# Gate and up of the second FFN by seven half-size products instead of eight, on normalised activations

## The chip, the cores and the metric

One core of a Trainium2 chip. The metric is the device time of one execution in microseconds (us), the median of several runs.

## The reference

One step of a decoder layer over 544 tokens: 512 of a prompt and 32 of eight decoding sequences.

```python
def rmsnorm(x, g):
    xf = x.astype(jnp.float32)
    y = xf * lax.rsqrt(jnp.mean(xf * xf, axis=-1, keepdims=True) + EPS)
    return (y * g.astype(jnp.float32)).astype(x.dtype)

def swiglu(x, w_gate, w_up, w_down):
    return (jax.nn.silu(x @ w_gate) * (x @ w_up)) @ w_down

x = x + 0.5 * swiglu(rmsnorm(x, ffn1_norm), ffn1_w_gate, ffn1_w_up, ffn1_w_down)
x = x + mixer(rmsnorm(x, mix_norm))     # convolution group and sparse attention group
x = x + 0.5 * swiglu(rmsnorm(x, ffn2_norm), ffn2_w_gate, ffn2_w_up, ffn2_w_down)
```

x has 1024 features, the hidden layer of an FFN 2816 = 22 x 128. Everything is float32.

## The kernel before

The activations lie transposed in SBUF, features on the partitions: x is [128, 8 k-tiles, 544 tokens]. A float32 product is made of three products in the format fp32r: each operand is split into a high part (ScalarE's copy rounds it) and a low part (VectorE subtracts the high part from the source), and high x high, high x low and low x high are accumulated in PSUM.

`stream` brings 128 columns of a weight matrix into one of three staging buffers (`wst`, `WB = 3`), and splits them into `whi` and `wlo` (L166, L171), which go round three slots of one buffer each. `wmm` then runs, for each of the 8 k-tiles, three kinds of product and two halves of the tokens (272 columns each): 48 matmuls for a unit of 128 hidden features.

`ffn` walks over the hidden tiles f = 0 to 21 in three blocks (`BLOCKS`: 8, 8 and 6 tiles). Within a block it makes, for each f, a gate unit G and an up unit U, and `hidden` evicts both with the factor R = 1 / root mean square of each token (L276: `t<-G,R`, `u<-U,R`), applies silu on ScalarE (L278), multiplies (L280) and splits the result into `hh` and `hl` (L281, L282). Then it runs the down projection of the block: 8 chunks Y of output features, each over the block's 6 or 8 hidden tiles, added to x by L330. In the first FFN the same code runs; the diff leaves that FFN alone.

Before the second FFN stands the output projection of the mixer, `w_out(1)`: 8 chunks Yo, added to x by L1236. After each chunk `done` squares it (`sq`, `S`) and splits it, with the norm's gain, into the `xh` and `xl` of the second FFN (L207, L208). The sum of squares is complete after the eighth chunk; `rms_from_S` and `spread` then give R on all partitions (L260). Since R scales the columns of a product, the units of f = 0 run before R is there.

The order of the instructions on each engine is fixed when the kernel is built: a scheduler takes, on each engine, the ready instruction that comes first in the program (with offsets for some parts). So G's matmuls of f = 0 lie among those of Yo. GpSimd does nothing in the second FFN.

After each output chunk of the last block `done2` transposes it (`yT`, `yS`), copies it out of PSUM (`yn`) and writes it to DRAM in pieces.

Of the kernel before, what the change touches and what calls it, by code (L numbers as in the profile page):

```python
# [7 lines left out]
F32 = mybir.dt.float32  # L8
# [49 lines left out]
KTB = 3  # L58
PSC = 1
# [58 lines left out]
class Trunk:  # L118
# [36 lines left out]
    def stream(self, srcs, n, m, kind="", slot=None):  # L155
        """fp32 weights [128, n, m] from DRAM, as the two float32r parts, in the given or the next place of three."""
# [25 lines left out]
    def wmm(self, unit, parts, act, cuts=HALVES, which=(0, 1)):  # L182
        """unit[:, i, :] = W^T act over all k-tiles, for the ith cut of the tokens; W stationary."""
# [10 lines left out]
    def fmm(self, name, parts, act, n):  # L194
        """two PSUM banks, one per half of the tokens: W^T act over n k-tiles."""
# [35 lines left out]
    def rms(self, ssq):  # L231
        """sums of squares [128 tokens, 5 tiles] -> rn, 1 / root mean square."""
# [19 lines left out]
    def spread(self):  # L252
        """R [128, T]: the row of rn on every partition."""
# [9 lines left out]
    def ffn(self, wg, wu, wd, done, late=False):  # L263
# [3 lines left out]
        def hidden(f, G, U):  # L267
            """G, U: one PSUM tile of equal halves, or (columns, PSUM) pairs."""
# [95 lines left out]
    def begin_units(self):  # L364
        """loads and transposes the activations; the first gate and up units, by halves of the tokens as these come in."""
        nc, tc, i = self.nc, self.tc, self.i
        with tc.tile_pool(name="init", bufs=1) as ip, tc.high_priority(offset=FIRST):
# [13 lines left out]
            def weights(w, n):  # L381
                """w's first 128 columns in n runs of k-tiles: for each a function that loads it, fp32 and the two parts."""
# [57 lines left out]
            def mms(unit, w, hf, order="01234567" * 2):  # L440
                """the high parts of the weights at a k-tile's first mention, the low ones at its second."""
# [112 lines left out]
    def rope(self, v, i, n, nh, kind):  # L554
        """partial rotary on v [n tokens, nh, 64] of token tile i."""
# [32 lines left out]
    def load_half(self, pieces, m, ks=(4, 4), slots=(0, 1)):  # L588
        """w_in columns in runs of ks k-tiles, [128, k, m] each; pieces: (offset in tile, first column, width)."""
# [717 lines left out]
    def mixer(self):  # L1307
        nc, tc, i = self.nc, self.tc, self.i
        self.idx_cols = [([(0, C_QI, 256)], 256), ([(0, C_QI + 256, 328)], 328, KS, (2, 0, 1))]
        with tc.tile_pool(name="mid", bufs=1) as mp:  # L1310
# [124 lines left out]
            for c, _ in enumerate(self.w_out(1, act)):  # L1435
                done(c)
# [79 lines left out]
```

## Time and profile before

| what | us |
|---|---|
| median of 3 runs | 1278.44 |
| lowest and highest of them | 1274.17, 1284.3 |
| span of the profiled execution, first to last instruction | 1270.2 |
| median of the runs less that span | 8.2 |
| second FFN in the profiled execution, G of f = 2 to the last Y | 890.3 to 1265.3 |

The profiled execution's own time is not listed beside its span; only the three runs have one. A row of the trace names the line of the kernel, the engine (PE TensorE, DVE VectorE, ACT ScalarE, POOL GpSimd), the operation, what is written from what, and its shape. Matmuls are pipelined: the record of one is longer than the distance to the next. DVE instructions overlap a little in the same way, so that the distance from start to start is the price in a queue.

### The profile page before, as it was taken

To read this page: it belongs to the slowest core of one execution; us is meant where nothing else is said; L and a number is where in the kernel's file an instruction comes from. 1 tells how busy PE (TensorE), PEld (TensorE's weight loads), DVE (VectorE), ACT (ScalarE), POOL (GpSimd) and SP (SyncE) were. 2 spreads that over 40 slices of the span, in tenths; PEclk is the share of its full clock that TensorE was granted. 3 is DMA by queue.
4 is the path that set the end of the run, shared out by engine and by line. 5 is a ranking of instruction groups with operands and counts; after the bars stand their busy time and mean duration, and the time that the engine had idled before them with its cause. 6 is when DMAs were issued, how large, how long until landed. Compare 5 with 4: busy or idle time off the path is not lost.

```text
span 1270.2 us, 22873 instructions
## 1 busy us (share of the span) xinstructions
PE 1230.0 (97%) x9629; PEld 1112.8 (88%) x9629; DVE 640.4 (50%) x1230; ACT 456.4 (36%) x696; POOL 209.3 (16%) x319
## 2 busy tenths in 40 slices
PE   9999999999999999899989989999999999999998
PEld 8999999999999747776667545789999999999998
DVE  5444334433446216999999753265443344433442
ACT  6332122212224464456525556244222122222222
POOL 3200000000000646665413231310000000000000
PEclk9999999999999999999999999999999999999999
DMA  7422332332222553245224443543223323322322
GB/s 231 133 85 84 93 90 84 92 92 84 86 73 69 179 178 106 68 138 169 68 61 140 161 151 124 167 141 113 87 84 93 91 84 87 96 85 84 91 75 74
DMA packets 184363, 136.10 MB, mean 107 GB/s; under 512 B 5706, under 2 KB 172434, under 8 KB 184260
## 3 DMA queue, kind: packets, MB, share of 16 engines
q1 hardware_dynamic: 171700, 91.62, 24.7%
q0 software_dynamic: 11904, 42.26, 10.3%
q8 instruction: 76, 1.25, 0.4%
q10 hardware_dynamic: 656, 0.76, 0.2%
q14 instruction: 27, 0.22, 0.1%
HBM read 131.66 MB, written 2.96 MB: 106 GB/s over the span
## 4 chain that ended last, share of the span: by engine, by line
PE 83%; DVE 10%; DMA 2%; issue 2%; ACT 1%; POOL 1%; DVEq 0%; ACTq 0%; POOLq 0%
PE Y L191 20%; PE U L191 20%; PE G L191 19%; PE Yo L130 4%; DVE flip L829 3%; PE KTp L134 2%; PE lg L130 2%; PE nat L130 2%; DMA ckn<-in_cache_k,ik 2%; PE O L130 2%; PE ssc L130 1%; PE plg L130 1%; PE pO L130 1%; DVE pw L928 1%; PE gc L130 1%
## 5 line engine op out<-in xcount | busy, mean ns | idle before, releaser
L166 ACT ACTIVATE whi<-wst 128x1024 fp32r<-128x1024 f32 (+3 forms) x173 | 172.7, 999 | 582.6 <-PE Y L191 181.2
L171 DVE TENSOR_TENSOR wlo<-wst,whi 128x1024 fp32r<-128x1024 f32 (+3 forms) x156 | 180.7, 1158 | 26.8 <-ACT whi L166 23.1
L191 PE MATMUL Y<-hh,wlo 128*128 128x272 f32 (+2 forms) x704 | 147.6, 288 | 0.0
L191 PE MATMUL Y<-hh,whi 128*128 128x272 f32 (+2 forms) x704 | 147.4, 289 | 0.0
L191 PE MATMUL Y<-hl,whi 128*128 128x272 f32 (+2 forms) x704 | 147.1, 288 | 0.0
L191 PE MATMUL U<-xh,whi 128*128 128x272 f32 x688 | 142.0, 287 | 1.5 <-DVE t L274 1.5
L191 PE MATMUL U<-xh,wlo 128*128 128x272 f32 x688 | 141.6, 288 | 0.0
L191 PE MATMUL U<-xl,whi 128*128 128x272 f32 x688 | 141.3, 287 | 0.0
L191 PE MATMUL G<-xh,whi 128*128 128x272 f32 x656 | 135.6, 287 | 0.0
L191 PE MATMUL G<-xl,whi 128*128 128x272 f32 x656 | 135.0, 287 | 0.0
L191 PE MATMUL G<-xh,wlo 128*128 128x272 f32 x656 | 134.9, 288 | 0.0
L276 DVE TENSOR_TENSOR u<-U,R 128x544 f32<-128x544 f32 x43 | 31.2, 725 | 160.2 <-PE U L191 160.2
L191 PEld LDWEIGHTS Y<-hl,whi 128*128 128x128 f32 x704 | 111.4, 188 | 0.0
L191 PEld LDWEIGHTS Y<-hh,whi 128*128 128x128 f32 x704 | 111.1, 188 | 0.0
L191 PEld LDWEIGHTS Y<-hh,wlo 128*128 128x128 f32 x704 | 110.7, 189 | 0.0
L330 DVE SCALAR_TENSOR_TENSOR x<-Y,x 128x544 f32<-128x544 f32 x46 | 33.3, 725 | 152.2 <-PE Y L191 152.2
L191 PEld LDWEIGHTS U<-xh,whi 128*128 128x128 f32 x688 | 107.1, 188 | 1.6 <-ACT whi L166 1.6
L191 PEld LDWEIGHTS U<-xl,whi 128*128 128x128 f32 x688 | 107.5, 188 | 0.0
L191 PEld LDWEIGHTS U<-xh,wlo 128*128 128x128 f32 x688 | 107.1, 189 | 0.0
L169 POOL TENSOR_TENSOR wlo<-wst,whi 128x1024 fp32r<-128x1024 f32 (+2 forms) x17 | 34.4, 2025 | 423.4 <-ACT whi L166 422.8
L191 PEld LDWEIGHTS G<-xl,whi 128*128 128x128 f32 x656 | 102.6, 188 | 0.0
L191 PEld LDWEIGHTS G<-xh,whi 128*128 128x128 f32 x656 | 102.2, 188 | 0.0
(330 smaller groups left out, 2235.0 us busy)
## 6 DMA issues: line engine op xcount, KB each, us to landing
wst<-in_ffn_w_up SPq DMA_DIRECT2D x44, 512.0 KB, 3.7
wst<-in_ffn_w_gate SPq DMA_DIRECT2D x43, 512.0 KB
wst<-in_ffn_w_down SPq DMA_DIRECT2D x32, 512.0 KB, 4.1
wst<-in_w_in SPq DMA_DIRECT2D x16, 512.0 KB, 4.0
wst<-in_ffn_w_down SPq DMA_DIRECT2D x16, 384.0 KB, 3.5
xn<-in_x_prompt SPq DMA_DIRECT2D x4, 512.0 KB
wst<-in_w_in SPq DMA_DIRECT2D x8, 256.0 KB, 8.9
wst<-in_w_out SPq DMA_DIRECT2D x8, 256.0 KB, 2.6
```

The costliest lines, as they stand in the source:

```text
L130: ins = self.nc.tensor.matmul(*args, **kw)
L134: ins = self.nc.tensor.transpose(*args)
L166: nc.scalar.activation(hi, st, AF.Copy)
L169: nc.gpsimd.tensor_tensor(lo, st, hi.bitcast(F32), op=ALU.subtract)
L171: nc.vector.tensor_sub(lo, st, hi.bitcast(F32))
L191: self.nc.tensor.matmul(unit[:, i, :c1 - c0], a[:, k, :], b[:, k, c0:c1], start=k == 0 and j == 0, stop=k == n - 1 and j == 2)
L276: nc.vector.tensor_mul(dst.rearrange("p (a b) -> p a b", a=2), src[:, :, :HT], self.R.rearrange("p (a b) -> p a b", a=2))
L330: nc.vector.scalar_tensor_tensor(xc, Y[:, :, :HT], 0.5, xc, op0=ALU.mult, op1=ALU.add)
L829: V.tensor_scalar(junk, src, cand[:, k:k + 1], None, op0=ALU.is_ge, op1=ALU.add, accum_out=cnt[:, k:k + 1])
L928: nc.vector.scalar_tensor_tensor(W, t, wcol, W, op0=ALU.mult, op1=ALU.add)
```

## The change

Gate and up of the second FFN get a function of their own, `ffn_late`. The tiles f = 0 and 1 are made as before. From f = 2 on two neighbouring tiles are made together: the weights of the pair are a 2 x 2 matrix of blocks (two tiles of hidden features, two halves of the 1024 input features), the activations another one (two halves of the input features, two halves of the tokens), and their product is made by the Winograd form of Strassen's algorithm, 7 products of 4 k-tiles and 272 columns in place of 8. `factors` loads the two tiles, builds four sums of weight blocks on GpSimd and splits the seven left factors. `right` multiplies the activations by the gain and by R (so that the pairs need no R at the eviction), forms four differences on GpSimd and splits the seven right factors, once. `unit` runs the products and adds them up. The three constants are SB = 1 (one buffer for the sums of weights), ZB = 1 (one for the results) and EVICT = "vector". The split activations of f = 0 and 1 move to the memory of `hh` and `hl`, the block of four right factors takes that of the mixer's `xh` and `xl`, and later the output tiles `yn` and `ys` take it.

```diff
+    def factors(self, srcs, nk):
...
+        (a11, a12), (a21, a22) = [(t[:, 0], t[:, 1]) for t in st]
+        def parts(src, n, eng):
+            slot, self.slot = self.slot, (self.slot + 1) % 3
...
+            nc.scalar.activation(hi, src, AF.Copy)
+            eng.tensor_tensor(lo, src, hi.bitcast(F32), op=ALU.subtract)
+            return [(hi[:, h], lo[:, h]) for h in range(n)]
+        p11, p12 = parts(st[0], 2, nc.vector)
+        s12, s34 = (self.fp.tile([128, 2, nk, 128], F32, name=n, tag=n, bufs=SB) for n in ("s12", "s34"))
+        for dst, a, b, op in ((s12[:, 0], a21, a22, ALU.add), (s12[:, 1], s12[:, 0], a11, ALU.subtract),
+                              (s34[:, 0], a11, a21, ALU.subtract), (s34[:, 1], a12, s12[:, 1], ALU.subtract)):
+            nc.gpsimd.tensor_tensor(dst, a, b, op=op)
+        p1, p2 = parts(s12, 2, nc.vector)
+        p3, p4 = parts(s34, 2, nc.vector)
+        p22, = parts(st[1][:, 1:2], 1, nc.vector)
+        return p11, p1, p2, p12, p3, p4, p22
+    def right(self, scale):
...
+        def row(r):
+            for k in range(n):
+                c, dst = r * n + k, v[:, r, k].rearrange("p c n -> p (c n)")
+                if r == 0:
+                    nc.vector.scalar_tensor_tensor(dst, self.x[:, c, :], scale[:, c:c + 1], self.R, op0=ALU.mult, op1=ALU.mult)
+                else:
+                    nc.scalar.activation(dst, self.x[:, c, :], AF.Copy, scale=scale[:, c:c + 1])
+                    nc.gpsimd.tensor_tensor(dst, dst, self.R, op=ALU.mult)
+        def split(i, src):
+            t, j = places[i]
+            for ks in both:
+                hi, lo = (a[:, j, ks] for a in t)
+                nc.scalar.activation(hi, src[:, ks], AF.Copy)
+                nc.vector.tensor_sub(lo, src[:, ks], hi.bitcast(F32))
+        def less(name, a, b):
+            t = fp.tile([128, n, HT], F32, name=name, tag=name, bufs=1)
+            for ks in both:
+                nc.gpsimd.tensor_tensor(t[:, ks], a[:, ks], b[:, ks], op=ALU.subtract)
+            return t
+        (b11, b12), (b21, b22) = [[v[:, r, :, c] for c in range(2)] for r in range(2)]
+        row(0)
+        split(0, b11)
+        t1 = less("t1", b12, b11)
+        split(1, t1)
+        row(1)
+        t2 = less("t2", b22, t1)
+        split(2, t2)
+        split(3, b21)
+        split(4, less("t1", b22, b12))
+        split(5, b22)
+        split(6, less("t1", b21, t2))
...
+    def unit(self, name, left, right, nk, z):
...
+        def product(n, out):
+            (wh, wl), (bh, bl) = left[n], right[n]
+            for k in range(nk):
+                for j, (w, b) in enumerate(((wh, bh), (wh, bl), (wl, bh))):
+                    nc.tensor.matmul(out, w[:, k, :], b[:, k, :], start=k == 0 and j == 0, stop=k == nk - 1 and j == 2)
+            return out
+        nc.scalar.activation(m1, product(0, self.funit(name)[:, :HT]), AF.Copy)
+        nc.scalar.activation(m5, product(1, self.funit(name)[:, :HT]), AF.Copy)
+        w = self.wunit(name)
+        V.tensor_add(z[:, 0], product(2, w[:, 0, :HT]), m1)
+        p = product(3, self.tunit(name)[:, :HT])
+        V.tensor_add(z[:, 3], p, m1)
+        V.tensor_add(z[:, 2], product(4, w[:, 1, :HT]), z[:, 0])
+        EV.tensor_tensor(z[:, 1::5], z[:, 0:3:2], m5[:, None, :].to_broadcast([128, 2, HT]), op=ALU.add)
+        w = self.wunit(name)
+        product(5, w[:, 0, :HT])
+        product(6, w[:, 1, :HT])
+        V.tensor_add(z[:, 4:6], w[:, :, :HT], z[:, 1:3])
+    def ffn_late(self, wg, wu, wd, done):
...
+        def hidden(f):
+            s, u = quarters("s"), quarters("u")
+            self.unit("G", cols(wg, f), xs, KC // 2, s)
+            nc.scalar.activation(s[:, 3:7], s[:, 3:7], AF.Silu)
+            self.unit("U", cols(wu, f), xs, KC // 2, u)
+            nc.vector.tensor_mul(u[:, 3:7], u[:, 3:7], s[:, 3:7])
+            return u
...
+                G = list(self.fmm("G", gp, act, KC))
+                xs = self.right(self.par[:, 16:24])
+                U = self.wunit("U")
+                self.wmm(U, self.cols(wu, 128, 128), act)
...
+            for k in range(0, nf, 2):
+                u = rows2(us if f0 + k == 0 else hidden(f0 + k))
+                for cut in (slice(0, 1), slice(1, 2)) if k == nf - 2 else (slice(0, 2),):
+                    hd = slice(k + cut.start, k + cut.stop)
+                    nc.scalar.activation(hh[:, hd], u[:, cut], AF.Copy)
+                    nc.vector.tensor_sub(hl[:, hd], u[:, cut], hh[:, hd].bitcast(F32))
```

## Rows read from the trace of the kernel before

**Rows 1.** The head of the page: busy time of each engine, and the span in 40 slices (busy tenths; PEclk is the granted clock of TensorE in tenths).

```profile
PE 1230.0 (97%) x9629; PEld 1112.8 (88%) x9629; DVE 640.4 (50%) x1230; ACT 456.4 (36%) x696; POOL 209.3 (16%) x319
PE   9999999999999999899989989999999999999998
POOL 3200000000000646665413231310000000000000
PEclk9999999999999999999999999999999999999999
```

**Rows 2.** The chain of work that ended last, in order of time, in the second FFN: start, length, what.

```profile
884.28 5.99 PE U L191 x48
890.27 5.97 PE G L191 x48
896.24 5.97 PE U L191 x48
...
955.97 5.97 PE U L191 x48
961.95 48.10 PE Y L191 x384
1010.05 5.97 PE G L191 x48
...
1099.64 5.97 PE U L191 x48
1105.61 48.10 PE Y L191 x384
1153.71 5.97 PE G L191 x48
...
1219.41 5.97 PE U L191 x48
1225.39 9.01 PE Y L191 x72
```

**Rows 3.** The timeline of VectorE, then of ScalarE, around the last up unit of the first block: start, length, line, operation, and in brackets the idle time before it and what ended it.

```profile
961.98 0.72 DVE L276 TENSOR_TENSOR u<-U,R 128x544 f32<-128x544 f32 x1 [3.85 <-PE U L191]
962.81 0.73 DVE L280 TENSOR_TENSOR u<-u,ts 128x544 f32<-128x544 f32 x1
963.46 1.22 DVE L171 TENSOR_TENSOR wlo<-wst,whi 128x1024 fp32r<-128x1024 f32 x1
964.59 0.72 DVE L282 TENSOR_TENSOR hl<-u,hh 128x544 fp32r<-128x544 f32 x1
...
955.81 1.06 ACT L166 ACTIVATE whi<-wst 128x1024 fp32r<-128x1024 f32 x1 [3.52 <-PE G L191]
```

**Rows 4.** The timeline of VectorE where R becomes ready.

```profile
878.29 0.69 DVE L260 COPY R<-rb 128x512 f32<-128x512 f32 x1 [2.38 <-PE rb L258]
878.90 1.22 DVE L171 TENSOR_TENSOR wlo<-wst,whi 128x1024 fp32r<-128x1024 f32 x1
880.03 0.72 DVE L276 TENSOR_TENSOR t<-G,R 128x544 f32<-128x544 f32 x1
880.67 0.71 DVE L276 TENSOR_TENSOR u<-U,R 128x544 f32<-128x544 f32 x1
881.31 0.44 DVE L274 TENSOR_TENSOR t<-G,R 128x272 f32<-128x272 f32 x1
881.66 0.72 DVE L280 TENSOR_TENSOR u<-u,ts 128x544 f32<-128x544 f32 x1
```

**Rows 5.** Groups of instructions of VectorE by line and shape, over the span: count, then busy us and mean ns of one.

```profile
L171 DVE TENSOR_TENSOR wlo<-wst,whi 128x512 fp32r<-128x512 f32 x10 | 6.9, 687 | 0.7 <-ACT whi L166 0.3
L208 DVE SCALAR_TENSOR_TENSOR xl<-x,par,xh 128x544 fp32r<-128x544 f32 x15 | 11.7, 778 | 0.0
```

**Rows 6.** Groups of instructions of GpSimd by line and shape, over the span, and two rows of its timeline.

```profile
L169 POOL TENSOR_TENSOR wlo<-wst,whi 128x1024 fp32r<-128x1024 f32 x10 | 24.4, 2444 | 8.8 <-ACT whi L166 8.3 <-issue 0.5
L169 POOL TENSOR_TENSOR wlo<-wst,whi 128x512 fp32r<-128x512 f32 x6 | 7.7, 1279 | 48.0 <-ACT whi L166 48.0
L958 POOL TENSOR_TENSOR R<-R 128x544 f32<-128x544 f32 x1 | 1.1, 1094 | 0.0
...
495.28 0.72 POOL L586 TENSOR_TENSOR nq<-nq,gq 128x256 f32<-128x256 f32 x1 [1.27 <-DVE nq L585]
496.08 0.32 POOL L564 TENSOR_TENSOR rp<-nq,main 128x64 f32<-128x64 f32 x1
```

**Rows 7.** The timelines of VectorE and GpSimd where instructions of both fall together, in four places.

```profile
847.09 0.72 DVE L226 TENSOR_TENSOR S<-S,sq 128x544 f32<-128x544 f32 x1
849.57 1.30 POOL L169 TENSOR_TENSOR wlo<-wst,whi 128x512 fp32r<-128x512 f32 x1 [13.58 <-ACT whi L166]
850.17 1.29 DVE L226 TENSOR_TENSOR S<-S,sq 128x544 f32<-128x544 f32 x1 [0.79 <-ACT sq L224]
...
538.41 2.45 POOL L169 TENSOR_TENSOR wlo<-wst,whi 128x1024 fp32r<-128x1024 f32 x1
538.53 2.35 DVE L847 TENSOR_TENSOR base<-base,add 128x1 f32<-128x1 f32 x1
...
446.30 1.21 DVE L171 TENSOR_TENSOR wlo<-wst,whi 128x1024 fp32r<-128x1024 f32 x1
446.31 1.37 POOL L564 TENSOR_TENSOR rp<-nq,main 128x64 f32<-128x64 f32 x1
...
581.80 2.36 POOL L169 TENSOR_TENSOR wlo<-wst,whi 128x1024 fp32r<-128x1024 f32 x1
582.08 0.43 DVE L1012 TENSOR_TENSOR yc<-gb,yc 128x272 f32<-128x272 f32 x1
```

**Rows 8.** Busy time of each engine in stretches of the mixer: stretch, length, then busy us and instructions of PE, PEld, DVE, ACT and POOL, the granted clock as a share, the DMA share and GB/s.

```profile
490.00:500.00 10.00, 7.12 (x60) 6.69 (x59) 8.51 (x24) 5.44 (x9) 7.37 (x14) 1.00 0.02 3
500.00:510.00 10.00, 8.85 (x68) 7.88 (x66) 9.69 (x27) 6.37 (x12) 7.20 (x12) 0.83 0.32 105
```

**Rows 9.** DMA issues: what is loaded, count, size of one, median us from issue to landing; and two issues on SyncE's queue in order of time.

```profile
wst<-in_ffn_w_up SPq DMA_DIRECT2D x44, 512.0 KB, 3.7
...
863.68 0.37 SPq L163 DMA_DIRECT2D wst<-in_ffn_w_gate  x1
869.13 0.37 SPq L163 DMA_DIRECT2D wst<-in_ffn_w_up  x1
```

More of the change, by code (lines that the diff above doesn't have):

```diff
@@ L58 @@
 KTB = 3
+SB = 1
+ZB = 1
+EVICT = "vector"
 PSC = 1
@@ L332, in ffn @@
                             done(c)
+    def factors(self, srcs, nk):
+        nc = self.nc
+        st = []
+        for load in srcs:
+            t = self.sp.tile([128, 2 * nk * 128], F32, name="wst", tag="wst", bufs=WB).rearrange("p (h k m) -> p h k m", h=2, k=nk)
+            for dst, src in load(t):
+                nc.sync.dma_start(dst, src)
+            st.append(t)
+        (a11, a12), (a21, a22) = [(t[:, 0], t[:, 1]) for t in st]
+        def parts(src, n, eng):
+            slot, self.slot = self.slot, (self.slot + 1) % 3
+            hi, lo = (self.sp.tile([128, n * nk * 128], F32R, name=nm, tag=f"{nm}{slot}", bufs=1).rearrange("p (h k m) -> p h k m", h=n, k=nk)
+                      for nm in ("whi", "wlo"))
+            nc.scalar.activation(hi, src, AF.Copy)
[10 more added lines that the diff above has]
+        return p11, p1, p2, p12, p3, p4, p22
@@ new lines, in right @@
+    def right(self, scale):
+        nc, fp, n = self.nc, self.fp, KC // 2
+        v = fp.tile([128, 2, n, 2, HT], F32, name="xn", tag="xn", bufs=1)
+        x3 = [fp.tile([128, 3, n, HT], F32R, name=nm, tag=nm, bufs=1) for nm in ("x3h", "x3l")]
+        x4 = [self.xp.tile([128, 4, n, HT], F32R, name=nm, tag=nm, bufs=1) for nm in ("xh", "xl")]
+        places = [(x3, 0), (x3, 1), (x3, 2), (x4, 0), (x4, 2), (x4, 1), (x4, 3)]
+        both = [slice(k, k + 2) for k in range(0, n, 2)]
+        def row(r):
[29 more added lines that the diff above has]
+        split(6, less("t1", b21, t2))
+        return [[a[:, j] for a in t] for t, j in places]
@@ new lines, in unit @@
+    def unit(self, name, left, right, nk, z):
+        nc = self.nc
+        V, EV = nc.vector, getattr(nc, EVICT)
+        m1, m5 = (self.fp.tile([128, HT], F32, name=n, tag=n, bufs=ZB) for n in ("m1", "m5"))
+        def product(n, out):
[16 more added lines that the diff above has]
+        V.tensor_add(z[:, 4:6], w[:, :, :HT], z[:, 1:3])
@@ new lines, in run, with done2 @@
+            out = {}
+            yp_out = o["y_prompt"][0].rearrange("(a p) d -> p a d", p=128)
+            def done2(c, part=None):
+                if c == 0:
+                    out["p"] = self.xp.tile([128, 4, D], F32, name="yn", tag="xh", bufs=1)
+                    out["s"] = self.xp.tile([NS, D], F32, name="ys", tag="xl", bufs=1)
+                yn, ys = out["p"], out["s"]
+                w = self.funit("yT").rearrange("p (a b) -> p a b", a=4)
+                tiles = range(5) if part is None else (range(3) if part == 0 else range(3, 5))
+                cs = slice(c * 128, (c + 1) * 128)
+                for t in tiles:
+                    c0, n = self.ntile(t)
+                    if t == 0:
+                        v = self.sunit("yS")
+                        nc.tensor.transpose(v[:NS, :128], self.x[:, c, :NS], self.ident)
+                    else:
+                        nc.tensor.transpose(w[:, t - 1, :], self.x[:, c, c0:c0 + 128], self.ident)
+                a = slice(max(tiles[0], 1) - 1, tiles[-1])
+                nc.scalar.activation(yn[:, a, cs], w[:, a], AF.Copy)
+                if tiles[0] == 0:
+                    nc.vector.tensor_copy(ys[:, cs], v[:NS, :128])
+                if c in (3, 5, 6, 7):
+                    h = slice({3: 0, 5: 4, 6: 6, 7: 7}[c] * 128, (c + 1) * 128)
+                    nc.sync.dma_start(yp_out[:, a, h], yn[:, a, h])
+                    if tiles[0] == 0:
+                        nc.scalar.dma_start(o["y_sample"].rearrange("b t d -> (b t) d")[:, h], ys[:, h])
@@ L1489 @@
+            self.ffn_late(i["ffn2_w_gate"][0], i["ffn2_w_up"][0], i["ffn2_w_down"][0], done2)
 _INS = ["x_prompt", "x_sample", "cache_k", "cache_v", "cache_idx_k", "cache_conv", "page_table",
```

101 lines of the change are left out of this document (68 added, 33 removed).

## The prediction

> **What bounds the kernel now.** I read the head of the page first: TensorE is busy 97% of the span, its granted clock is full in every slice, and GpSimd does nothing in the last third [rows 1]. Then the chain of waits: from 884 us to the end of the second FFN it is matmuls alone, with no gap, 5.97 us for a unit of 48, so 124.4 ns for one of 272 columns [rows 2]. No load, eviction or split is late there. So a matmul taken away is worth its 124.4 ns, as long as the other engines keep up; the question is whether they do.
>
> **Matmuls removed.** A pair of tiles needs 4 x 48 = 192 matmuls for gate and up; seven products of 4 k-tiles and 3 kinds, twice, are 168. Ten pairs (f = 2 to 21) lose 24 each: 240 x 0.1244 = 29.9 us. Shape and number of weight loads per matmul stay, so I take the same pace. A pair then costs TensorE 20.9 us (before 23.9), one Strassen unit 10.45, one product 1.493.
>
> **Prices.** VectorE's rows overlap by some 0.08 us, so I take the distance from start to start: 544 columns 0.65 (962.81 to 963.46), 1024 columns 1.13 (963.46 to 964.59) [rows 3], 272 columns out of PSUM 0.35, 544 out of PSUM 0.64 [rows 4]; 512 columns 0.687 - 0.08 = 0.60, a scaled 544 0.69 [rows 5]; 1088 columns, by the step from 512 to 1024, 1.20. For GpSimd's 512-column sum in plain float32 there is no row. From below: 544 columns took 1.094, but there both inputs are the same tensor, so 1.03. From above: 1.28 for 512 columns that are written as fp32r. Plain float32 with two different inputs took 0.32 for 64 columns and 0.72 for 256, a slope of 2.1 ns a column, hence 1.25 for 512, which I take, and 1.33 for 544 [rows 6].
>
> **Work added to a pair.** VectorE, per unit: low parts of three 1024s and one 512 (3 x 1.13 + 0.60 = 3.99), one sum of SBUF tiles (0.65), three small adds and one large one out of PSUM (3 x 0.35 + 0.64 = 1.69). Per pair, with the product of gate and up and the split of the result (2 x 1.20): 15.1 us, where 20.9 are there. ScalarE has less (3 x 1.06 for the high parts [rows 3] and half of that once more per unit, and the result): some 11 of 20.9. GpSimd: 8 sums, 10.0. None of the engines alone is a bound.
>
> **Two engines, one port.** Together VectorE and GpSimd are. In the mixer, wherever a VectorE instruction with two inputs in SBUF starts under one of GpSimd's, it ends only after GpSimd's: S<-S,sq takes 1.29 instead of 0.72 and ends 0.59 after GpSimd's end at 850.87; a sum of one column takes 2.35 and ends with GpSimd's at 540.86. The other way too: GpSimd's 64 columns take 1.37 instead of 0.32 [rows 6] when VectorE's split started just before. With one input in PSUM, VectorE isn't held: 0.43 at 582.08 [rows 7]. The page "SBUF — State Buffer" of the Trainium skill (Who interferes with whom) states this as a rule: a VectorE instruction with two SBUF inputs and a GpSimd instruction that reads SBUF exclude each other for the whole instruction. The trace agrees, with the rows just named.
>
> So per pair the port carries VectorE's two-input work, 2 x 4.64 + 2.40 = 11.7, and GpSimd's 10.0: 21.7 us against TensorE's 20.9 and 23.9 before. With the low price of GpSimd (1.03) it would be 19.9. The page "GPSIMD Engine Reference" (3.1 Elementwise) has 4497 ns for 2048 columns, by which I estimate 1.12 for 512: the port would then carry 20.7 and lie just under TensorE. My rows give the larger price, and I go by them.
>
> **The start.** R is there at 878.9 [rows 4], and the plain units of f = 1 occupy TensorE until 890.27; the first Strassen unit would reach its seventh product 6 x 1.493 later, at 899.2. Until then the port must carry: the split of f = 1's up weights 1.13, two gate-up products 1.30, the first half of the activations 4 x 0.69 = 2.76, seven splits in two halves 14 x 0.65 = 9.10, low parts of the weights 2.86, one sum 0.65, and on GpSimd 4 multiplications by R and 8 differences, 12 x 1.33 = 15.96. Sum 33.8: the seventh product starts at 912.7, 13.4 us late. The sums of the first weights (5.0) are free: before, the two loads in their place go out at 863.68 and 869.13 and take 3.7 [rows 9], so GpSimd can add from 873 on; if the first waits for R, add 5. For the rest of block 0 the port still has 1.2 (split of the first pair), 9.6 (second unit), 2.4 and 43.4 (two pairs) less 2.4 behind the last matmul: 54.2, to 966.9, where the kernel before is at 961.95 [rows 2]. Lost there: 5 us if the port never idles, 9.5 if it idles 5% of the 88; I take 8.
>
> **Blocks 1 and 2.** During the 48 us of Y the port is nearly free, so the first unit's sums (5.0) and two of its low parts (2.3) are ready, and 2.4 come after the last matmul. Block 1 needs 4 x 21.7 - 9.7 = 77.1 of the port, TensorE 83.6, before 95.56 [rows 2]: TensorE bounds it again, by a little. Block 2: 55.4 against 62.7, before 71.7. To this come jitters. The tightest place is the ring of three weight slots, since a pair's unit takes four: the second set of the next unit goes into the slot that the sixth product frees, and is due two products later (2.99, and 0.25 more for the low part). High and low part take 2.33 from the first one's start (955.81, as with 1.06, 0.04 and 1.23) and some 0.16 for the matmul's end: 2.5 of 3.24. A GpSimd sum in the way costs up to 1.25, so a stall of 0 to 0.5, and 0 to 1.2 where VectorE's order puts the gate-up product first. I take 0.4 for each of 14 units: block 1 gains 12.0 - 3.2 = 8.8, block 2 9.0 - 2.4 = 6.6.
>
> **Small things.** Down projections and the end are the same work. The last pair's result needs sum, product, copy and split, some 3.7 us, where the six-tile block needs it after 4 x 0.75 = 3.0: 0.5. Loads: two of 512 KB per 10.45 us and 3.7 to land [rows 9]; a staging buffer comes back after four sums, 5.0 + 3.7 = 8.7 of 10.45, so hidden, but a GpSimd that is held 0.5 us per sum uses the slack up (0 to 1 us a unit, in the jitter's upper end). The memory moves cost nothing: the new tiles replace what was read before (the mixer's operands ahead of `w_out(1)`'s end, the right factors 9 us ahead of the first `yn`); without that cover it would be tenths.
>
> **Sum.** +8 - 8.8 - 6.6 + 0.5 = -7 us: span 1263, and by the median, which lies 8.2 above the span, 1271.5. Its own range: port never idle and GpSimd at its low price -17, jitters at their upper end +6, so 1261 to 1284. About 1% (13 us) is what a measurement of this kernel can tell from no change; the forecast lies within it.
>
> **Rivals.** *The port doesn't serialise in practice*: GpSimd's sums fall under VectorE's waits and PSUM reads, and the start is bounded by VectorE alone. Against it stand [rows 7], for it the low price [rows 6]. Then the start has 17.8 of the 33.8, with 2.6 and 1.7 of PSUM reads 22.1, to 901.0, 2 us late; jitters 20 x 0.2 = 4; -29.9 + 2 + 4 + 0.5 = -23: 1255. *VectorE's queue adds GpSimd's time to its own*: it takes its instructions in a fixed order, so a PSUM read behind a held instruction waits too, at L276's place, and little of it falls under GpSimd. A pair then costs 15.1 + 10.0 = 25.1, more than the 23.9 before. The PSUM reads add 3.6 in the start and 8.5 behind it: block 0 ends at 979 (+17), block 1 takes 100.4 - 9.7 = 90.7 (-5), block 2 65.6 (-6): +6, and with 8% idle +25, +3 and 0, so +28; in the middle +17: 1295. It decides from the point where a pair costs more than 23.9. For it: both held instructions of [rows 7] wait to GpSimd's very end. Against it: most reads come while sums run, since these are half of a unit. *The ring of slots*: the eviction (0.64) and the gate-up product (1.20) always ahead of the second set's low part, 1.1 us at each of ten pairs: +4, 1282. *A clock step*: TensorE waits half of the start; in the mixer a stretch with 7.12 of 10 us busy is followed by one at 0.83 [rows 8]. Up to 10 x 0.17 = 1.7 a time, in the ranges.
>
> **Chances.** Forecast 0.41, no serialising 0.26, added queue 0.27, ring 0.06. Faster by over 1%: 0.26 and a fifth of the forecast's, 0.35. Slower by over 1%: most of the added queue's, 0.23. Within: 0.42. The range leaves out the lower part of 1255's case and the upper third of 1295's: 1252 to 1298.
>
> **What would show it.** Right: 240 matmuls fewer, TensorE still at 124 ns within a product; GpSimd sums of about 1.25 that end together with stretched VectorE subtractions; the first Strassen unit stretched to some 24 us from 890, and block 0's Y starting after 962; short waits for wlo in blocks 1 and 2. Wrong: if Y of block 0 starts before 958, the start was over-sized; if units of block 1 take over 11.9, the queue is the bound; if GpSimd's sums are far from 1.25, or VectorE's instructions aren't stretched under them, the port's sum falls.

## The result, and the profile after

The changed kernel takes 1287.97 us (median of 5 runs, 1287.03 to 1289.46) where the kernel before takes 1279.19 (5 runs, 1274.17 to 1284.3): a ratio of 1.0073, 95% interval 1.0051 to 1.0096. The prediction was 1271.5, range 1252 to 1298. The time is in the range, but on the other side: a loss of some 9 us stands where 7 us of gain were forecast.

The head of the page of the changed kernel, the lines that answer to [rows 1] and VectorE's:

```profile
PE 1215.8 (95%) x9383; PEld 1091.9 (85%) x9389; DVE 752.5 (59%) x1330; ACT 509.2 (40%) x776; POOL 369.9 (29%) x411
...
PE   8999999999999998899879989999699999999998
...
DVE  5444344333347208998998743267977368744772
...
POOL 3200000000001636664412232306552156403620
PEclk9999999999999999999999999999899999999999
```

TensorE issues 246 matmuls fewer by the records (240 by the code; some records are missing in a trace) and is busy 14 us less; yet the span grew. VectorE, at 3 or 4 tenths in the second FFN before, is now at 6 to 9 wherever gate and up are made.

Where the time went is read by stages, from marks that both kernels have: the last transpose of the attention's output (OT, ahead of `w_out(1)`; up to there the order of the instructions is the same), the copy of R, and the first and last matmul of Y in each block. I start at OT because the work ahead of it differs between executions: OT stands at 836.6 us in the profile of before, at 843.1 in that of after, and at 836.7 to 843.9 in those of the experiments. The last line is what TensorE alone would need, at 1.493 us for a product.

| us | OT to R | R to Y of block 0 | Y | gate/up block 1 | Y | gate/up block 2 | Y | end | sum |
|---|---|---|---|---|---|---|---|---|---|
| before | 41.7 | 83.5 | 48.3 | 95.4 | 48.3 | 71.5 | 40.1 | 4.9 | 433.6 |
| after | 43.6 | 98.1 | 48.4 | 90.6 | 49.9 | 67.3 | 40.7 | 4.6 | 443.1 |
| difference | +1.9 | +14.6 | +0.1 | -4.8 | +1.6 | -4.2 | +0.6 | -0.3 | +9.5 |
| TensorE alone | | 74.5 | | 83.6 | | 62.7 | | | |

The +9.5 agrees with the medians' +8.8. So blocks 1 and 2 gain 9.0 us, under half of the 20.6 that the matmuls would give, and block 0 loses more than both gain.

The groups of GpSimd and VectorE behind 860 us, shapes apart (count, then busy us and mean ns of one, then idle time before and its enders):

```profile
L362 POOL TENSOR_TENSOR s<-wst 128x512 f32<-128x512 f32 x40 | 65.2, 1643 | 201.8 <-DMA wst<-in_ffn_w_gate 122.1 <-DVE wlo L355 45.8 <-DMA wst<-in_ffn_w_up 16.1
L362 POOL TENSOR_TENSOR s<-wst,s 128x512 f32<-128x512 f32 x20 | 38.6, 1932 | 1.0
L362 POOL TENSOR_TENSOR s<-s,wst 128x512 f32<-128x512 f32 x20 | 35.0, 1752 | 1.3
...
L355 DVE TENSOR_TENSOR wlo<-wst,whi 128x512 fp32r<-128x512 f32 x20 | 18.5, 924 | 0.1
L505 DVE TENSOR_TENSOR hl<-u,hh 128x1088 fp32r<-128x1088 f32 x8 | 17.5, 2189 | 0.4 <-ACT hh L504 0.4
L472 DVE TENSOR_TENSOR u<-u,s 128x1088 f32<-128x1088 f32 x10 | 20.5, 2054 | 0.1
L381 DVE SCALAR_TENSOR_TENSOR xn<-x,par,R 128x544 f32<-128x544 f32 x4 | 7.4, 1904 | 0.0
```

A sum was priced at 1.25 us; the shortest 26 of the 80 take 1.27 to 1.30, the mean of all is 1.74. On VectorE the 512 columns that took 687 ns before [rows 5] take 924, and a scaled 544, 778 before, takes 1904.

How they come to this, in the timelines of both engines within block 1 (start, length, line, what):

```profile
1057.36 3.27 POOL L362 TENSOR_TENSOR s<-wst 128x512 f32<-128x512 f32 x2 [4.04 <-DMA wst<-in_ffn_w_up]
1060.71 2.22 POOL L362 TENSOR_TENSOR s<-s,wst 128x512 f32<-128x512 f32 x1
1063.01 2.16 POOL L362 TENSOR_TENSOR s<-wst,s 128x512 f32<-128x512 f32 x1
...
1059.41 2.37 DVE L472 TENSOR_TENSOR u<-u,s 128x1088 f32<-128x1088 f32 x1
1061.88 0.44 DVE L429 TENSOR_TENSOR s<-G,m 128x272 f32<-128x272 f32 x1
1062.24 0.43 DVE L431 TENSOR_TENSOR s<-G,m 128x272 f32<-128x272 f32 x1
1062.59 1.43 DVE L355 TENSOR_TENSOR wlo<-wst,whi 128x1024 fp32r<-128x1024 f32 x1
1063.94 2.38 DVE L505 TENSOR_TENSOR hl<-u,hh 128x1088 fp32r<-128x1088 f32 x1
```

Read the ends. The pair of sums ends at 1060.63; u<-u,s, begun at 1059.41, ends 1.15 later, at 1061.78. The sum begun at 1060.71 ends 1.15 after that, at 1062.93. The low part begun at 1062.59 ends 1.09 later, 1064.02; the next sum 1.15 later, 1065.17; hl 1.15 later, 1066.32. In this stretch the two engines take strict turns, and each is shown busy while it waits. The two reads of PSUM (L429, L431) take their usual 0.44. They stand behind the held u<-u,s and can't begin before it has ended, but then they run while GpSimd is at the sum begun at 1060.71.

The chain of the last end, for a stretch of block 1 (start, length, what):

```profile
1069.07 3.45 POOL s L362 x2
1072.52 0.07 issue
1072.59 1.30 POOL s L362
1073.89 0.07 issue
1073.96 2.16 POOL s L362
1076.12 0.02 issue
1076.13 3.98 DMA wst<-in_ffn_w_up
...
1080.27 3.17 POOL s L362 x2
```

Before, this chain was matmuls without a gap [rows 2]. Now it goes round a loop: four sums in 7.1 us, a staging buffer comes free, its load takes 4.0, the next sums: 11.2 us a unit (1069.07 to 1080.27) where TensorE needs 10.45. From 1057.36 to 1080.27 a whole pair takes 22.9. In the stretch ahead of this one, from 1054.44 to 1069.02, the chain is VectorE's own queue with the held instructions shown above, and GpSimd's first sums of the unit wait for a low part there, which frees a buffer of the sums:

```profile
1069.07 3.44 POOL L362 TENSOR_TENSOR s<-wst 128x512 f32<-128x512 f32 x2 [3.90 <-DVE wlo L355]
```

The chain at the start of the second FFN, and the timelines of GpSimd, VectorE and TensorE there:

```profile
875.61 3.62 DMA wst<-in_ffn_w_gate
...
879.85 4.75 POOL s L362 x3
884.60 1.18 POOL rn L242
```

```profile
887.52 7.16 POOL L384 TENSOR_TENSOR xn<-xn,R 128x544 f32<-128x544 f32 x4 [0.49 <-DVE R L263]
...
889.69 7.38 DVE L381 SCALAR_TENSOR_TENSOR xn<-x,par,R 128x544 f32<-128x544 f32 x4
...
900.30 0.29 PE L423 MATMUL G<-xh,whi 128*128 128x272 f32 x1
904.63 0.60 PE L423 MATMUL G<-x3h,whi 128*128 128x272 f32 x1 [4.04 <-DVE s L456]
905.02 0.43 PE L423 MATMUL G<-x3l,whi 128*128 128x272 f32 x1
905.25 0.43 PE L423 MATMUL G<-x3h,wlo 128*128 128x272 f32 x1
```

Three sums of the first weights stand ahead of rn in GpSimd's queue, and R is made from rn. Then the multiplications by R, four on GpSimd and four on VectorE, hold each other: 7.38 us for VectorE's four, where [rows 5] give 2.8 for four (the 0.69 of the prediction). TensorE begins the first Strassen unit at 898.5 and makes its last matmul at 930.0, 31.5 us later; 39 matmuls of the second unit (4.9 us) lie among them, which leaves 26.6 where 24 were expected.

### The profile page after: what moved, and what is told of

Its sections match the earlier page's. It is cut to its first block, busy times and chain, and to the rows that moved or that the text cites. A ratio compares the mean times of both kernels' runs of the same rounds, so it can differ in the third digit from the quotient of the medians.

```text
span 1286.2 us, 22759 instructions
## 1 busy us (share of the span) xinstructions
PE 1215.8 (95%) x9383; PEld 1091.9 (85%) x9389; DVE 752.5 (59%) x1330; ACT 509.2 (40%) x776; POOL 369.9 (29%) x411
## 4 chain that ended last, share of the span: by engine, by line
PE 64%; DVE 19%; POOL 6%; DMA 5%; issue 4%; ACT 2%; DVEq 0%; ACTq 0%; POOLq 0%
PE Y L194 20%; PE U L194 10%; PE G L194 10%; POOL s L362 5%; PE Yo L133 4%; DVE flip L1020 3%; PE KTp L137 2%; DVE wlo L355 2%; PE lg L133 2%; PE G L423 2%; PE nat L133 2%; DMA ckn<-in_cache_k,ik 2%; PE O L133 1%; PE U L423 1%; PE ssc L133 1%
## 5 line engine op out<-in xcount | busy, mean ns | idle before, releaser
L174 DVE TENSOR_TENSOR wlo<-wst,whi 128x1024 fp32r<-128x1024 f32 (+3 forms) x116 | 133.4, 1150 | 29.8 <-ACT whi L169 26.9
L362 POOL TENSOR_TENSOR s<-wst 128x512 f32<-128x512 f32 x40 | 65.2, 1643 | 201.8 <-DMA wst<-in_ffn_w_gate 122.1
L194 PE MATMUL U<-xh,whi 128*128 128x272 f32 x336 | 69.4, 288 | 1.9 <-DVE t L277 1.9
L194 PE MATMUL U<-xh,wlo 128*128 128x272 f32 x336 | 69.2, 288 | 0.0
L194 PE MATMUL U<-xl,whi 128*128 128x272 f32 x336 | 69.0, 287 | 0.0
L194 PE MATMUL G<-xh,whi 128*128 128x272 f32 x320 | 66.2, 288 | 0.0
L194 PE MATMUL G<-xh,wlo 128*128 128x272 f32 x320 | 65.9, 288 | 0.0
L194 PE MATMUL G<-xl,whi 128*128 128x272 f32 x320 | 65.8, 287 | 0.0
L355 DVE TENSOR_TENSOR wlo<-s,whi 128x1024 fp32r<-128x1024 f32 x40 | 50.3, 1258 | 17.4 <-ACT whi L354 17.4
L194 PEld LDWEIGHTS U<-xh,whi 128*128 128x128 f32 x336 | 52.3, 188 | 2.1 <-ACT whi L169 2.1
```

Source lines behind the costliest of these rows:

```text
L174: nc.vector.tensor_sub(lo, st, hi.bitcast(F32))
L194: self.nc.tensor.matmul(unit[:, i, :c1 - c0], a[:, k, :], b[:, k, c0:c1], start=k == 0 and j == 0, stop=k == n - 1 and j == 2)
L355: eng.tensor_tensor(lo, src, hi.bitcast(F32), op=ALU.subtract)
L362: nc.gpsimd.tensor_tensor(dst, a, b, op=op)
```

## The experiments

Stages as above; "one time" stands beside the one time of before that was taken with it. Most of these kernels have one execution; the stages of y_vec_ring2_start repeat within 0.3 us in a second one (92.5, 87.2, 64.5, in all 428.8).

| us | R to Y of block 0 | block 1 | block 2 | OT to end |
|---|---|---|---|---|
| before | 83.5 | 95.4 | 71.5 | 433.6 |
| after | 98.1 | 90.6 | 67.3 | 443.1 |
| x_no_sums | 91.4 | 85.6 | 63.9 | 424.6 |
| x_sums_vec | 91.9 | 95.4 | 66.7 | 438.2 |
| x_start_vec | 92.8 | 90.9 | 67.0 | 437.1 |
| x_ring | 102.5 | 89.2 | 65.8 | 441.8 |
| y_gp_ring2_start | 96.9 | 87.8 | 65.1 | 436.0 |
| y_mixed_ring2_start | 97.0 | 87.7 | 67.6 | 438.3 |
| y_vec_ring2_start | 92.2 | 87.2 | 64.5 | 429.2 |
| z_unused | 99.2 | 90.3 | 66.1 | 442.8 |
| v_no_sums_start | 84.6 | 85.5 | 63.9 | 418.9 |
| v_late | 86.4 | 90.7 | 67.0 | 428.3 |
| v_late_vec_ring2_start | 83.8 | 89.0 | 64.7 | 421.9 |

**What the sums cost: x_no_sums.**

```diff
-        s12, s34 = (...)
-        for dst, a, b, op in (...):
-            nc.gpsimd.tensor_tensor(dst, a, b, op=op)
-        p1, p2 = parts(s12, 2, nc.vector)
-        p3, p4 = parts(s34, 2, nc.vector)
+        p1, p2 = parts(st[1], 2, nc.vector)
+        p3, p4 = parts(st[0], 2, nc.vector)
```

> Left out: the four sums of weight blocks of each pair (the plain blocks are split in their place), so GpSimd does nothing in the units after the start. In the changed kernel the gate and up stretches of blocks 1 and 2 take 90.6 and 67.3 us (from the last Y of one block to the first Y of the next), where TensorE alone needs 83.6 and 62.7. If GpSimd's sums are what holds the units up (by the port, by the queue, or by the ring of staging buffers), the stretches fall to 84 to 86 and 63 to 65. If the ring of three weight slots does it, they stay within 1.5 us of 90.6 and 67.3. The start keeps its work on GpSimd: the first two Strassen units stay long (over 30 us together, where TensorE needs 20.9).

One time 1269.39 beside 1276.85. The stages are 18.5 us shorter than those of after: 1.9 of them at R (41.7 again, as before), 6.7 in block 0, 5.0 and 3.4 in blocks 1 and 2, 1.5 in the Y of block 1. VectorE's work is the same, but its instructions have their own length again; its group of the product of gate and up (mean ns):

```profile
L468 DVE TENSOR_TENSOR u<-u,s 128x1088 f32<-128x1088 f32 x10 | 12.9, 1287 | 0.1
```

In after this group (L472, above) has a mean of 2054. So the sums on GpSimd are the larger part of the loss, but not all of it: block 0 is still 7.9 us over before.

**The same sums on VectorE: x_sums_vec.**

```diff
-            nc.gpsimd.tensor_tensor(dst, a, b, op=op)
+            nc.vector.tensor_tensor(dst, a, b, op=op)
```

> The four sums of weights go from GpSimd to VectorE: 8 x 0.60 a pair, so VectorE has 19.9 us of the 20.9 that TensorE needs for a pair, and nothing shares the port in the units. All theories that blame GpSimd expect block 1 at 84 to 88 and block 2 at 63 to 66; if a VectorE that is busy 95% in a fixed order is as bad as the port, 89 or more and 66 or more. The start changes little (under 3 us).

One time 1283.86 beside 1276.85. Block 0 is as short as with no sums at all (91.9, 6.2 less than in after, where under 3 was expected), R is 0.5 us later than before; block 1 takes 95.4, all gain gone. Its chain in block 1:

```profile
1044.86 1.14 DVE wlo L355
1046.00 0.02 issue
1046.02 4.52 DMA wst<-in_ffn_w_up
...
1050.66 0.69 DVE s L362
...
1053.18 7.29 PE G L423 x44
```

A load now stands between two VectorE instructions: the low part frees the staging buffer, the load into it takes 4.52, and the sum that waits for it heads VectorE's queue, with everything behind it.

**The start's work on VectorE: x_start_vec.**

```diff
-                if r == 0:
-                    nc.vector.scalar_tensor_tensor(dst, self.x[:, c, :], scale[:, c:c + 1], self.R, op0=ALU.mult, op1=ALU.mult)
-                else:
-                    nc.scalar.activation(dst, self.x[:, c, :], AF.Copy, scale=scale[:, c:c + 1])
-                    nc.gpsimd.tensor_tensor(dst, dst, self.R, op=ALU.mult)
+                nc.vector.scalar_tensor_tensor(dst, self.x[:, c, :], scale[:, c:c + 1], self.R, op0=ALU.mult, op1=ALU.mult)
...
-                nc.gpsimd.tensor_tensor(t[:, ks], a[:, ks], b[:, ks], op=ALU.subtract)
+                nc.vector.tensor_tensor(t[:, ks], a[:, ks], b[:, ks], op=ALU.subtract)
```

> The multiplications by R and the differences of the activations go from GpSimd to VectorE (4 x 0.69 and 8 x 0.65 for 12 x 1.33, and ScalarE's four copies go); the units keep their sums on GpSimd. Port theory of the start: 33.8 us of the port become 25.8, so block 0 ends about 8 us earlier than the 98.1 us after R (886.7 to 984.8) that the changed kernel takes; blocks 1 and 2 stay at 90.6 and 67.3. If the start is bounded by something else (weights, the clock step at 904 to 909), under 3 us.

One time 1280.64 beside 1276.85: block 0 is 5.3 us shorter where some 8 were expected, blocks 1 and 2 are as in after. VectorE has twelve instructions more in the start, and its last split of a right factor ends 35.1 us behind R instead of 40.1.

**More staging buffers: x_ring.** The scratch `v` of the right factors is made of four tiles of a common tag with six buffers; the second staging tile of each load (from the third call on) and the sums go round in them.

```diff
+    def extra(self, name):
+        return self.fp.tile([128, 2 * T], F32, name=name, tag="extra", bufs=6)
...
-            t = self.sp.tile([128, 2 * nk * 128], F32, name="wst", tag="wst", bufs=WB)...
+            t = self.extra("wst")[:, :1024] if self.loads > 4 and self.loads % 2 == 0 else ...
```

> Same work on the same engines; the activations' scratch is made of four tiles that afterwards serve, with the sums' two, as a ring of six buffers: the second staging tile and the two sums of each unit go round in it. So a load no longer waits until GpSimd has ended the sums of the unit before, and a sum no longer until the one before is split. Ring theory (four held sums of 7.7 us and a load of 3.9 in a loop of 11.4 per unit): block 1 falls from 90.6 to 84 to 87, block 2 from 67.3 to 63 to 65. Queue theory (VectorE adds GpSimd's time to its own, 25.1 a pair less the head start): both stay within 1.5 us. Port theory (21.7 a pair without idle time): block 1 86 to 88, block 2 64 to 66.

One time 1283.15 beside 1276.85. The loop of sums and load appears in the chain from 1050 to 1091 us only once (a load of 3.65 and two sums), and yet blocks 1 and 2 gain only 1.4 and 1.5 us, what was expected if VectorE's queue bounds them, not if the ring does: what stands on the chain otherwise is VectorE's own queue with its held instructions. In block 0 it loses 4.4; the buffers are the memory that the right factors are still made from there, which would explain it, but I didn't test that. The loop, taken for the cause when the trace of after was first read, is one of two bounds of almost the same length.

**Combinations with GpSimd, mixed, and VectorE alone.** All have the start's work on VectorE, and a variant of the ring (ring2: four buffers for the second staging tile, and from the fourth call on every second pair of sums in the memory of `t1` and `t2`). They differ in who sums: GpSimd, GpSimd and VectorE by halves (`s12` and `s34`), VectorE.

> Two edits together: the activations' multiplications and differences on VectorE, and more buffers made of memory that is idle after the start (four for the second staging tile, two for each sum of weights); the sums stay on GpSimd. The one-edit runs gave 92.8 us from R to the first Y (start on VectorE), and 89.2 and 65.8 us for blocks 1 and 2 (ring of six). Ring theory, if six buffers were too few because the second staging tile is held until late in its unit: blocks 1 and 2 at 84 to 86 and 63 to 64.5. Port or queue theory: 87 to 90 and 65 to 67.

> As the run with start on VectorE and more buffers, with the first two sums of a unit on GpSimd and the last two on VectorE: VectorE 17.5 us of 20.9 a pair, the port 11.7 + 2.4 + 5.0 = 19.1. Port theory (its sum decides): block 1 84 to 86, block 2 63 to 64.5, better than either pure version. Queue theory (VectorE's work plus GpSimd's time, 17.5 + 5.0 = 22.5, against 25.1 and 19.9): between the two pure versions, near 86.

> As the run with start on VectorE and more buffers, with the sums of weights on VectorE too: GpSimd does nothing behind R. VectorE has 19.9 us of 20.9 a pair. With the sums on VectorE alone block 1 took 95.4 us, with waits for staging loads of 3.9 to 5.2 us on the chain (VectorE stands in order behind a sum whose load isn't there). If those loads were the cause, 84 to 87 for block 1 and 63 to 65 for block 2, and R to the first Y 84 to 89; if a VectorE at 95% can't be kept in step, 89 or more.

One time each, beside 1273.99: 1279.8, 1278.8 and 1274.28. With buffers enough, VectorE alone is best in each stage, by 4.7 us in block 0 and 0.6 in each of the others. The half and half split is no faster than GpSimd alone: 87.7 and 67.6 in blocks 1 and 2, where its port sum of 19.1 us a pair had let 84 to 86 and 63 to 64.5 be expected.

**Held or waited for: z_unused.** As y_gp_ring2_start, but the sums are made and not used: the four middle factors are split from the weights as loaded. So nothing but the freeing of staging buffers can wait for a sum.

```diff
-        p1, p2 = parts(s12, 2, nc.vector)
-        p3, p4 = parts(s34, 2, nc.vector)
+        p1, p2 = parts(st[1], 2, nc.vector)
+        p3, p4 = parts(st[0], 2, nc.vector)
```

> The kernel with start on VectorE and more buffers, where GpSimd makes the sums of weights and nobody uses them (left out: the sums in the product; the plain blocks are split in their place). So GpSimd is as busy as before, but no split waits for it. If a late sum is what costs (ring, or sums held by VectorE), block 1 falls to the 85.6 us of the run without sums, and block 2 to 63.9. If VectorE's instructions that are held under GpSimd's cost (port, queue), both stay within 1 us of the run with the sums in use, at 87 or more and 65 or more.

One time 1288.21 beside 1273.99. Blocks 1 and 2 take 90.3 and 66.1, 4.7 and 2.2 more than x_no_sums and 4.8 and 2.2 more than v_no_sums_start (below), which have the same splits, no sums and fewer buffers; the second has the start's work on VectorE too. From 1045 to 1110 us, in block 1, no GpSimd instruction and no load lies on its chain; VectorE's held ones do. The product of gate and up, 1287 ns without sums:

```profile
L481 DVE TENSOR_TENSOR u<-u,s 128x1088 f32<-128x1088 f32 x10 | 17.2, 1724 | 0.1
```

So it needs no wait for a sum: holding VectorE is enough for such a loss. Nor is it the port's sum: VectorE's instructions without a PSUM operand and GpSimd's together fill 69.3 of block 1's 90.3 us here. Why the kernel that does use its sums (y_gp_ring2_start) is faster by 2.5 us in block 1 stays open.

**No GpSimd at all: v_no_sums_start.** x_no_sums and x_start_vec together.

> Leaves out the sums of weights (their parts are split from the weights as loaded, so those products are not the reference's), and makes the multiplications by R and the differences of the start on VectorE: GpSimd does nothing behind rn. Theory that sums and start work hold VectorE independently: their effects add, R to first Y 98.1 - 6.7 - 5.3 = 86 us, block 1 85.6, block 2 63.9, near 1264 to 1265. Rival that VectorE's own fixed order bounds the start once the sums are gone: R to first Y stays at 90 to 92, as without the sums alone, near 1269.

One time 1257.38 beside a median of 1276.97; by the stages behind OT, which came early at 836.7, it is 418.9 against 433.6. R to Y of block 0 takes 84.6; adding the two single effects to after gives 98.1 - 6.7 - 5.3 = 86.1. So they add to within 1.5 us, and what is left of VectorE's own work in the start costs block 0 1.1 us against before. From VectorE's timeline, the multiplications by R:

```profile
882.30 5.65 DVE L376 SCALAR_TENSOR_TENSOR xn<-x,par,R 128x544 f32<-128x544 f32 x8
```

Eight on VectorE in 5.65 us; four on each engine took 7.38. With GpSimd's share the whole took longer than with VectorE doing all of it.

**The start under Y: v_late.** Block 0 stays plain, the right factors are made behind its last up unit, Strassen begins with block 1. 72 of the 240 matmuls come back.

```diff
-                G = list(self.fmm("G", gp, act, KC))
-                xs = self.right(self.par[:, 16:24])
...
+                if f0 == 0 and k:
+                    us = quarters("u")
+                    for r in range(2):
+                        G, U = self.wunit("G"), self.wunit("U")
+                        self.wmm(G, self.cols(wg, 128 * (k + r), 128), act)
+                        self.wmm(U, self.cols(wu, 128 * (k + r), 128), act)
+                        first_hidden(us, G, U, r)
+                u = rows2(us if f0 == 0 else hidden(f0 + k))
...
+            if f0 == 0:
+                xs = self.right(self.par[:, 16:24])
```

> Block 0 of the second FFN stays plain (all eight tiles as before the change, R at the eviction), and the right factors are made behind its last up unit, so that their work falls into the 48 us of block 0's Y; pairs by Strassen only in blocks 1 and 2, their sums on GpSimd as in the change. 72 of the 240 matmuls saved come back (9.0 us). Theory that the loss sits in the start, where the port's work stands against matmuls, and that blocks 1 and 2 keep their gains: from R to the first Y of block 0 83.5 to 84.5 us as before, Y of block 0 at most 2 us longer, block 1 about 90.6, block 2 about 67.3, so 8 us faster than before (near 1269 to 1271). Rival that the start's work is only moved and doesn't fit beside Y's own splits and evictions: block 1 starts late and takes 96 to 99, so no change or slower than before (1277 to 1282).

1270.31 us (10 runs) against 1276.97 (18 runs): 0.9952, interval 0.9930 to 0.9974. Blocks 1 and 2 are as in after; block 0 is 11.7 us shorter than in after, though it has 9.0 us of matmuls more. It is 2 us longer than expected because the scheduler still puts the multiplications by R as early as R allows: GpSimd's four take 7.14 us from 882.05, VectorE's four 7.36 from 884.23, and TensorE waits 1.6 for u behind them.

**Both cures: v_late_vec_ring2_start**, v_late with all of GpSimd's added work on VectorE and the buffers of ring2.

> As v_late, with all of the added work of GpSimd on VectorE (sums of weights, multiplication by R, differences) and the further staging buffers. Theory that holding by GpSimd is what the blocks still lose: block 0 83.5 to 84.5, its Y 48.4, block 1 about 87.2 and block 2 about 64.5 as with the same parts and Strassen from f = 2 on: 15 us faster than before, near 1262 to 1265. Rival that VectorE has too much in the 48 us of Y (some 15 us of splits and evictions, some 25 of the start): block 1 takes 91 or more, 1268 or more.

1264.52 us (4 runs) against 1276.97: 0.9915, interval 0.9898 to 0.9931, faster than both kernels. Its chain shows block 0 and its Y as in [rows 2], and GpSimd's page line is at its 209.3 us of before [rows 1]:

```profile
PE 1213.9 (96%) x9461; PEld 1095.2 (87%) x9461; DVE 730.1 (58%) x1371; ACT 496.5 (39%) x751; POOL 209.3 (17%) x319
```

```profile
952.81 6.00 PE G L195 x48
958.81 6.00 PE U L195 x48
964.81 47.83 PE Y L195 x384
...
1049.69 7.32 PE U L432 x56
1057.01 9.04 PE G L432 x72
```

Block 1 takes 89.0, not 87.2: the first pairs still wait for loads and sums (a load of 5.08 us at 1020.37 is on the chain). That part of the expectation was wrong.

**Strassen from f = 2 on, VectorE alone, timed: y_vec_ring2_start_t**, the kernel of y_vec_ring2_start.

> The kernel of y_vec_ring2_start again (Strassen from f = 2 on, all of GpSimd's work on VectorE, further staging buffers), timed against the kernel before. From the stages of its first trace (429.2 against 433.6 us from the last transpose of the mixer to the end): 3 to 5 us faster than before, a ratio of 0.996 to 0.998. If the start's loss differs from execution to execution: no change within 2 us.

1271.81 us (9 runs) against 1276.97: 0.9966, interval 0.9952 to 0.9979. So moving GpSimd's work away, with the buffers that this needs, turns the change from 0.7% slower to 0.3% faster; putting the start under Y gives 0.5% more.

## Why the prediction was wrong

Of the 16.5 us between the -7 that were forecast and the +9.5 of the stages, some 8.5 lie in block 0 and ahead of R, 6.4 in blocks 1 and 2, and 1.5 in Y and the end.

**The port's idle time. This is the step that failed.** The prediction let the longer of the port and TensorE decide, with 0.4 us a unit for all waits in blocks 1 and 2 ("TensorE bounds it again, by a little") and 3 us of idle port in block 0 (8 taken, 5 with a port that never idles). The port's work itself came out as forecast. From the records, the time in which a VectorE instruction without a PSUM operand or one of GpSimd's runs or is held:

| us | port forecast | port measured | stretch takes | port not used | TensorE alone |
|---|---|---|---|---|---|
| R to Y of block 0 | 88.0 | 87.3 | 98.1 | 10.9 | 74.5 |
| block 1 | 77.1 | 75.2 | 90.6 | 15.4 | 83.6 |
| block 2 | 55.4 | 53.6 | 67.3 | 13.7 | 62.7 |
| pair from 1057.36 | 21.7 | 21.2 | 22.9 | 1.7 | 20.9 |

So behind the first Strassen unit neither sum is the bound. Over TensorE's 10.45 a unit takes 0.9 us more in block 1 and 0.8 in block 2, not 0.4. The prices held too: an undisturbed sum takes 1.27 to 1.30 us (forecast 1.25), and VectorE's undisturbed ones are those of the sum, 1.29 for 1088 columns (forecast 1.20, as a distance from start to start, which is some 0.08 less than the length).

What the runs show in its place is the order of the instructions. An instruction of VectorE that is held for some 1.1 us (2.37 instead of 1.29 in the lines above) delays all that stands behind it, splits and PSUM reads, and with them matmuls; GpSimd's next sums wait for a load or for a low part, and the port stands unused meanwhile. x_no_sums brings 85.6 and 63.9, better than my forecast of 86.6 and 64.9 with sums; z_unused shows that the holding alone takes this away. How the unused time divides among these waits was not measured.

The rival that adds GpSimd's time to VectorE's queue came near in numbers: -5 and -6 us for blocks 1 and 2, where -4.8 and -4.2 were measured, and in all +6 without idle time and +28 with 8% of it, where +9.5 was measured. That is luck in part. Its pair was to cost 25.1 us, because little of the PSUM reads falls under sums; but in the pair above 3.0 of their 3.9 us do, and 8.5 of 15.7 in the whole of block 1. It was right that a read behind a held instruction waits.

The page "SBUF — State Buffer" of the Trainium skill (Who interferes with whom) has the exclusion of the two engines for the length of an instruction; the turns in block 1, each 1.09 to 1.15 us from the other's end, agree with it.

The page "GPSIMD Engine Reference" of the Trainium skill (3.1 Elementwise), from whose 4497 ns for 2048 columns I had estimated 1.12 us for a sum, lies below the 1.27 to 1.30 of the trace; the measurement decides.

**The start: 8 us forecast, 14.6 measured, and 1.9 more before R.** Three terms of it:
- The start's work was taken as a port that is filled almost without gaps. Up to the end of the first Strassen unit it was (42.4 of 43.4 us from R on), with sums and low parts of the second unit among it that the forecast had put behind the 33.8. From there to Y the port carried 44.9 us in 54.7. The experiments split the 14.6: VectorE alone 1.1 (v_no_sums_start), GpSimd's multiplications and differences some 6.8 more (x_no_sums), the sums 6.7 more (after). The rival's value for the end of block 0 was +17; the measured 14.6 + 1.9 is nearest to it.
- "The sums of the first weights are free" failed. Their second load went out at 875.61, as far behind OT (32.5 us) as the 869.13 of [rows 9], and GpSimd began to add when forecast. But three of the sums stand ahead of rn in its queue, which I hadn't counted among those they are moved past: rn begins 41.5 us behind OT, 38.2 before. R is 1.9 us later by it; in x_no_sums it is where it was before.
- Half speed: after the wait of 4.04 us the next 17 matmuls come 0.226 us apart instead of 0.125, and 12 more after the next long wait: 2.9 us. It was named in the ranges (1.7 a time) and not in the sum.

**Block ends.** I had 0.5 us for the last pair's result. In block 1 TensorE waits 1.79 for u, and 15 of the first 22 matmuls of Y run at half speed, 1.5 us; that half speed is Y's +1.6.

**Loads.** The loop was in the working as 8.7 of 10.45 us, with the remark that sums held by 0.5 use up the slack. They were held by 0.46 on average, and the loop took 11.2, so the remark was right, and what it costs was left out of the sum. What the loop costs by itself is less than its 0.75 us over TensorE: in x_ring, without most of it, a unit of block 1 is 0.2 us shorter, since VectorE's queue bounds it then.

**What was right.** The matmuls removed, at 124 to 125 ns; the port's sum; held subtractions and sums on both engines; Y of block 0 starting late. Of the signs that I had named as proof of an error one appeared, sums far from 1.25 (1.74 in the mean, though the undisturbed ones are near it). A unit of block 1 took 11.45 us in the pair above, under the 11.9 that I had named as the queue's mark; that mark, half of the 23.9 that a pair cost before, was set too high: VectorE's queue can stand on the chain, as here, and still leave a part of the gain.

**The offset of 8.2 us** was misread but did no harm. The profiled execution of after took 1288.36 for a span of 1286.2, so only some 2 us lie around a span; that of before was a quick one ahead of the second FFN. Since the forecast was the median less 7, the number is the same.

## What to carry to other kernels

Work given to GpSimd beside a busy VectorE isn't free: where both read two operands from SBUF they took turns here, and VectorE's fixed order passes the wait on to what stands behind. So the sum of what both put on the port is only the least that such a split takes (21.2 of the 22.9 us of a pair, 87.3 of 98.1 in block 0): look for the waits in each engine's order, and measure whether VectorE alone isn't faster (here 8 multiplications took 5.65 us on it, and 4 + 4 took 7.38). A scheme that saves matmuls by elementwise work pays where that work has cover: block 0 lost 14.6 us with the right factors made in front of its pairs, and 2.9 or, with VectorE alone, 0.3 with them behind its last unit, though waiting for that place gave 72 of the 240 matmuls back. When an engine takes over work that starts with a load, give it the buffers first (95.4 us for block 1 without, 87.2 with them).

## What the runs showed of the hardware

TensorE's clock after a wait, by stretches (length, then busy us and count of PE, PEld, DVE, ACT, POOL, granted clock, DMA share, GB/s), at the start and at block 1's Y of the changed kernel:

```profile
904.00:910.00 6.00, 5.37 (x24) 5.19 (x25) 6.00 (x9) 3.18 (x5) 3.05 (x3) 0.54 0.00 0
910.00:916.00 6.00, 4.37 (x31) 3.71 (x29) 6.00 (x5) 1.60 (x3) 6.00 (x4) 1.00 0.01 3
```

```profile
1123.75 0.49 PE L194 MATMUL Y<-hh,whi 128*128 128x272 f32 x2 [1.79 <-DVE u L432]
...
1118.00:1122.00 4.00, 3.97 (x32) 3.75 (x30) 1.23 (x1) 1.70 (x3) 0.00 (x0) 1.00 0.63 188
1124.00:1128.00 4.00, 4.00 (x22) 4.00 (x22) 3.39 (x4) 0.51 (x1) 0.00 (x0) 0.57 0.77 220
1128.00:1132.00 4.00, 4.00 (x34) 4.00 (x34) 1.36 (x2) 0.70 (x2) 0.00 (x0) 1.00 0.16 47
```

The granted clock is 0.54 over the 6 us from 904, around the end of a wait of 4.04 us, and 0.57 over the 4 us from 1124, behind a wait of only 1.79 us that followed a busy stretch at full clock: near half, the 1.2 GHz level of the two. It doesn't fall with every such wait. In v_late this one is followed by matmuls at 0.125:

```profile
900.83 0.49 PE L194 MATMUL U<-hh,whi 128*128 128x272 f32 x2 [1.60 <-DVE u L458]
```

What decides was not tested.
